# Three quarters of w_down in seven block products in place of eight

## The chip, the cores and the metric

The kernel runs on one core of one Trainium2 chip. The metric is the device time of one execution in microseconds; of several runs the median counts. The engines are TensorE (PE), VectorE (DVE), ScalarE (ACT), GpSimd (POOL) and SyncE (SP); matmuls write to PSUM, everything else of the work lies in SBUF, and weights come from HBM by DMA.

## The reference

One step of a hybrid decoder layer for 512 prompt tokens and 8 x 4 sample tokens (544 columns in all): two recurrent branches, a gated merge, an output projection, then an MLP and a last norm. Only the MLP is touched.

```python
D_MODEL = 1024
D_FF = 4 * D_MODEL
...
    h2 = _rmsnorm(x, norm_mlp_g)
    x = x + jnp.square(jax.nn.relu(h2 @ w_up)) @ w_down
...
    y = _rmsnorm(x, norm_final_g)
```

All data is float32.

## The kernel before

Activations lie channel-major: a tile has 128 channels on the partitions and the 544 tokens as columns, in two halves of 272 (HALF). To keep float32 accuracy every operand is split into two parts for the matmul, hi (rounded, by ACT) and lo (the difference, by DVE), and a product is the sum of three: hi x hi, lo x hi, hi x lo.

The unit of work is `full_unit`: `load8` (SP, L177) brings 128 columns of a weight, [128, 8, 128] = 512 KB, into a stage tile `st` (4 buffers), `split` makes `whi` (ACT, L132, 3 buffers) and `wlo` (DVE, L135, 2 buffers), and 48 matmuls (L129: 3 pairs of parts x 8 tiles of 128 rows x 2 halves of the columns) fill one `pd` tile, which has two PSUM banks. The pool of these has two tiles, so the next unit runs while this one is read out.

The MLP goes through the hidden rows in two halves and a rest. For each of e = 0, 1 there are 16 up units; of each DVE makes `r` = max(ps, 0) * rsb (L138, one operation for each half of the columns), ACT squares it and makes `hd` hi, DVE `hd` lo. Then come the products with w_down for 8 output tiles x2[j] of 128 channels (names x in the trace): in e = 0 two units of 8 hidden tiles each, in e = 1 one unit, and DVE adds the sum to x2[j] (two operations of 272). The last quarter of the hidden rows (3072 and up) follows apart: its weights are kept as `wkh`, `wkl`, and each part of the tokens is finished with the last norm while the next products run.

So w_down takes 24 units of 48 matmuls for the first three quarters. Each engine runs its instructions in the order of its own stream; waits between engines are semaphores. Loads are issued by SP as soon as a stage buffer is free.

Of the kernel before, what the change touches and what calls it, by code (L numbers as in the profile page):

```python
# [20 lines left out]
NSMP = NB * NT  # L21
# [15 lines left out]
NS_M = 43  # L37
# [23 lines left out]
def hybrid_step(ctx: ExitStack, tc: tile.TileContext, i, o):  # L61
# [47 lines left out]
    class Lane:  # L109
        """slots and PSUM banks of one of the two background lanes"""  # L110
# [32 lines left out]
    def rsq(x, scale=None, eps=None):  # L143
        """x <- (x * scale + eps) ** -0.5 of a few columns: a guess from the exponent, three Newton steps"""
# [67 lines left out]
    def stats(t):  # L212
        """1 / rms of every token of a tile, on every partition"""
# [52 lines left out]
    class Late:  # L266
        """Pool operations that stay behind those already queued"""
# [17 lines left out]
    def consts1():  # L285
# [5 lines left out]
        # masks of the RWKV pair products, rows s, columns t: [A_vk^T | A_re^T] over [A_zb^T (negated) | A_rb^T]  # L291
# [27 lines left out]
    def consts3():  # L319
        # sample masks: same sequence, strictly causal towards kk, causal towards r  # L320
# [9 lines left out]
        # rows of a sequence: bmk[row, b]  # L330
# [216 lines left out]
    def rw_batch(pairs, xk, xr, xv):  # L547
        """channel-major preparation and the pair products of two head pairs"""
# [211 lines left out]
    def rw_chain(g):  # L760
        """the state from chunk to chunk, and the outputs"""
# [57 lines left out]
    def gn(y, ng, S):  # L819
        """zero mean, unit variance over the 64 values of each (token, head); y: [128, ng, 64]"""  # L820
# [31 lines left out]
    def rw_state(L, p):  # L852
        """sample states of a head pair, transposed to [(h, key), b, value]"""
# [12 lines left out]
    def rw_sample(L):  # L866
        """four tokens of eight sequences; rows (head of the pair, key side | value side, token)"""
# [297 lines left out]
    def hg_sample(L):  # L1165
        """four tokens of eight sequences, four heads; columns and rows (head, sequence, token)"""
# [27 lines left out]
        # exact parts stacked along the rows: k = [hi; lo; hi], v = [hi; hi; lo]  # L1194
# [180 lines left out]
    psm = ctx.enter_context(tc.tile_pool(name="psm", bufs=2, space=bass.MemoryType.PSUM))  # L1375

# [52 lines left out]
    def row_scale():  # L1429
        """1/sqrt(mean + eps) of every token on every partition"""  # L1430
# [96 lines left out]
    for e in range(2):  # L1527
        hd_hi, hd_lo = [], []
        for f in range(16):
            ps = full_unit(i["w_up"][0], 2048 * e + 128 * f, xg_hi, xg_lo,  # L1530
                           late=2 * (e == 0 and f == 0))[:, :, 0:HALF]
            if e == 0 and f == 0:
                row_scale()
            r = Y(TOK, name="r")
            for b in range(2):
                stt(r[:, HALF * b:HALF * b + HALF], ps[:, b], 0.0, rsb[:, HALF * b:HALF * b + HALF], ALU.max, ALU.mult)
            act(r, r, AF.Square)
            for c, hd in enumerate((hd_hi, hd_lo)):
                slot = M if f < 9 else O if 2 * f + c < 18 + NS_O else Y
                hd.append(slot(TOK, F32R, "hd"))  # L1540
            act(hd_hi[f], r)
            tt(hd_lo[f], r, hd_hi[f].bitcast(F32), ALU.subtract)
# [69 lines left out]
```

## Time and profile before

| | |
|---|---|
| median of 3 runs | 1001.56 us (999.77 to 1001.76) |
| span of the profiled execution, first to last instruction | 996.1 us |
| PE busy | 962.8 us, 97% |
| DVE busy | 584.3 us, 59% |
| ACT busy | 394.0 us, 40% |
| POOL busy | 135.8 us, 14% |

The profiled execution is known by its span alone; the runs' times are some 5 us above it. The stages from 560 us on are, by the chain that ended last: up units to 692, w_down of e = 0 to 789, up units of e = 1 to 885, then w_down of e = 1 and the last quarter. A busy share is an average over stages; what matters for the change are the stages from 604 to 934 us.

### The profile page before, as it was taken

To read this page: it belongs to the slowest core of one execution; us is meant where nothing else is said; L and a number is where in the kernel's file an instruction comes from. 1 tells how busy PE (TensorE), PEld (TensorE's weight loads), DVE (VectorE), ACT (ScalarE), POOL (GpSimd) and SP (SyncE) were. 2 spreads that over 40 slices of the span, in tenths; PEclk is the share of its full clock that TensorE was granted. 3 is DMA by queue.
4 is the path that set the end of the run, shared out by engine and by line. 5 is a ranking of instruction groups with operands and counts; after the bars stand their busy time and mean duration, and the time that the engine had idled before them with its cause. 6 is when DMAs were issued, how large, how long until landed. Compare 5 with 4: busy or idle time off the path is not lost.

```text
span 996.1 us, 21327 instructions
## 1 busy us (share of the span) xinstructions
PE 962.8 (97%) x8868; PEld 908.1 (91%) x8868; DVE 584.3 (59%) x1198; ACT 394.0 (40%) x722; POOL 135.8 (14%) x328
## 2 busy tenths in 40 slices
PE   5999999999999899999999999999999999999996
PEld 4999988889998886888899999999999999999995
DVE  6635979578696854679878554444222244445333
ACT  7554545514636441334444333333111233333232
POOL 4486423221132101101000000000000000000000
PEclk9999999999999899999999999999999999999998
DMA  9632343222345232445743642322223332234111
GB/s 273 173 105 81 81 91 100 57 66 90 114 107 109 44 107 63 124 135 171 256 122 128 197 128 84 87 85 86 85 86 89 97 90 86 86 106 142 50 44 48
DMA packets 191091, 106.38 MB, mean 107 GB/s; under 512 B 38945, under 2 KB 179047, under 8 KB 190994
## 3 DMA queue, kind: packets, MB, share of 16 engines
q1 hardware_dynamic: 165424, 95.16, 32.8%
q10 hardware_dynamic: 25570, 9.85, 3.9%
q8 instruction: 70, 1.15, 0.5%
q14 instruction: 27, 0.22, 0.1%
HBM read 85.08 MB, written 18.39 MB: 104 GB/s over the span
## 4 chain that ended last, share of the span: by engine, by line
PE 81%; DVE 9%; DMA 4%; ACT 3%; POOL 2%; issue 1%; SPq 1%; ACTq 0%; DVEq 0%; POOLq 0%
PE pd L129 24%; PE in_unit_ps L129 20%; PE full_unit_ps L129 19%; PE half_unit_ps L129 4%; PE rw_chain_pq L129 2%; DVE tmp L135 2%; PE rw_chain_py L129 1%; DVE wlo L135 1%; PE rw_out_pt L129 1%; PE rw_sample_pn L129 1%; PE hg_head_po L129 1%; PE lora_ps L129 1%; DVE bn L724 1%; DMA xin<-in_x_prompt_dram 1%; PE hg_head_pl L129 1%
## 5 line engine op out<-in xcount | busy, mean ns | idle before, releaser
L132 ACT ACTIVATE whi<-st 128x1024 fp32r<-128x1024 f32 x120 | 126.7, 1057 | 251.6 <-PE pd L129 119.2
L135 DVE TENSOR_TENSOR wlo<-st,whi 128x1024 fp32r<-128x1024 f32 x120 | 149.2, 1244 | 126.0 <-PE full_unit_ps L129 40.3
L129 PE MATMUL in_unit_ps<-h_hi,whi 128*128 128x272 f32 (+3 forms) x736 | 121.3, 300 | 2.3 <-ACT h_hi L132 1.4
L129 PE MATMUL in_unit_ps<-h_hi,wlo 128*128 128x272 f32 (+3 forms) x736 | 121.7, 299 | 0.0
L129 PE MATMUL in_unit_ps<-h_lo,whi 128*128 128x272 f32 (+3 forms) x736 | 121.2, 300 | 0.0
L129 PEld LDWEIGHTS in_unit_ps<-h_hi,whi 128*128 128x128 f32 x736 | 103.3, 194 | 8.4 <-issue 3.4
L129 PE MATMUL full_unit_ps<-hd,whi 128*128 128x272 f32 (+2 forms) x832 | 110.3, 289 | 0.0
L129 PEld LDWEIGHTS in_unit_ps<-h_hi,wlo 128*128 128x128 f32 x736 | 103.2, 193 | 4.4 <-issue 2.4
L129 PEld LDWEIGHTS in_unit_ps<-h_lo,whi 128*128 128x128 f32 x736 | 103.7, 194 | 3.8 <-issue 1.9
L129 PEld LDWEIGHTS full_unit_ps<-hd,whi 128*128 128x128 f32 x832 | 106.5, 188 | 0.0
L129 PE MATMUL pd<-xgl,whi 128*128 128x272 f32 x512 | 70.2, 289 | 0.0
L129 PE MATMUL pd<-xgh,wlo 128*128 128x272 f32 x512 | 69.8, 288 | 0.0
L129 PE MATMUL pd<-xgh,whi 128*128 128x272 f32 x512 | 69.8, 288 | 0.0
L141 POOL TENSOR_SCALAR ys<-ys,ssf 32x512 f32<-32x512 f32 x1 | 0.8, 830 | 491.1 <-DVE ssf L1495 491.1
L129 PEld LDWEIGHTS pd<-xgl,whi 128*128 128x128 f32 x512 | 66.7, 188 | 0.0
L129 PEld LDWEIGHTS pd<-xgh,whi 128*128 128x128 f32 x512 | 66.2, 188 | 0.0
L129 PEld LDWEIGHTS pd<-xgh,wlo 128*128 128x128 f32 x512 | 66.2, 188 | 0.0
L129 PE MATMUL full_unit_ps<-hd,wlo 128*128 128x272 f32 (+2 forms) x416 | 56.8, 288 | 0.0
L129 PEld LDWEIGHTS full_unit_ps<-hd,wlo 128*128 128x128 f32 x416 | 54.0, 188 | 0.0
L135 DVE TENSOR_TENSOR hd<-r,hd 128x544 fp32r<-128x544 f32 x32 | 23.2, 725 | 47.9 <-ACT hd L132 47.9
L135 DVE TENSOR_TENSOR x<-x,full_unit_ps 128x272 f32<-128x272 f32 (+2 forms) x48 | 19.5, 434 | 36.9 <-PE full_unit_ps L129 36.9
L138 DVE SCALAR_TENSOR_TENSOR r<-pd,rsb 128x272 f32<-128x272 f32 x64 | 25.2, 435 | 25.9 <-PE pd L129 23.9
(413 smaller groups left out, 1500.9 us busy)
## 6 DMA issues: line engine op xcount, KB each, us to landing
st<-in_w_in_dram SPq DMA_DIRECT2D x46, 512.0 KB
st<-in_w_up_dram SPq DMA_DIRECT2D x32, 512.0 KB
st<-in_w_down_dram SPq DMA_DIRECT2D x32, 512.0 KB
gt_d<-gt SPq DMA_DIRECT2D x16, 272.0 KB
st<-in_w_out_dram SPq DMA_DIRECT2D x8, 512.0 KB
gtb<-gt_d SPq DMA_DIRECT2D x8, 272.0 KB
gta<-gt_d SPq DMA_DIRECT2D x8, 272.0 KB
x<-xt_d SPq DMA_DIRECT2D x8, 272.0 KB
```

The lines of the kernel that those rows point to most:

```text
L129: T.matmul(out, lhsT, rhs, start=start, stop=stop)
L132: A.activation(out=out, in_=in_, func=func, **kw)
L135: (eng or V).tensor_tensor(out=out, in0=a, in1=b, op=op)
L138: V.scalar_tensor_tensor(out=out, in0=a, scalar=s, in1=b, op0=op0, op1=op1)
L141: (eng or V).tensor_scalar(out=out, in0=a, scalar1=s1, scalar2=s2, op0=op0, op1=op1)
L724: V.tensor_reduce(out=o_[:, i0:i1, t0:t1], in_=tp, axis=AX.X, op=ALU.add)
```

## The change

The three quarters of the hidden rows 0 to 3071 are taken one after the other. Within a quarter each pair of hidden tiles (two of 128 rows), each pair of output tiles and the two halves of the tokens make a product of 2 x 2 blocks, and this is done by the scheme of Winograd with seven block products and sums of operands in place of eight. A block product is 12 matmuls of 272 columns (3 pairs of parts x 4 hidden pairs), and `down(c, ops, jp)` does the seven products for quarter c and output pair jp: 84 matmuls where there were 96.

- The sums of activations (`bt`, `t23`, `t4`) are made in `even` and `odd` behind the up units, and their parts take the place of those of the plain hidden values.
- The sums of weights (`sx`, in place in `st`, `s4`) are made in `down_weights` from two loads: t2 (odd hidden tiles) and t1 (even ones), each in two DMAs of 256 KB on SP. w1, w3 and w4 are split by ACT and DVE as before. Of w2, which is t2 as loaded, ACT makes hi, then a negated copy of it in the new tile `slo`, and a DMA issued by POOL adds t2 to that copy.
- Products 1 and 5 share a `pd` tile, 6 and 7 the next; these sums are kept over the quarters in `acc` (eight tiles of 544), written by ACT in c = 0 and added to by DVE after. Products 2 and 3 are added to one x2 tile at once, product 4 is subtracted from the other. Once, with c = 2, `combine(jp)` brings the kept sums into x2 by six DVE operations.
- One up unit of the next quarter runs ahead of the downs of each quarter.
- The last quarter (`plain`, and what follows) is as before. Pools: NS_M from 43 to 44, a pool `sp` for `slo` (2) and `sx` (1), `gs` moved to another pool. Docstrings and comments are left out.

```diff
-    for e in range(2):
-        hd_hi, hd_lo = [], []
-        for f in range(16):
...
-        for j in range(8):
-            ps = pd("full_unit_ps")
-            for kb in range(2 - e):
-                full_unit(i["w_down"][0], 128 * j, hd_hi[8 * kb:8 * kb + 8], hd_lo[8 * kb:8 * kb + 8], ps,
-                          kb == 0, kb == 1 - e, 2048 * e + 1024 * kb)
-            for b in range(2):
-                r = slice(HALF * b, HALF * b + HALF)
-                tt(x2[j][:, r], x2[j][:, r], ps[:, b, 0:HALF], ALU.add)
...
+    def even(r):
+
+        bt, t23 = Y(TOK, name="bt"), Y(TOK, name="t23")
+        act(bt[:, lh], r[:, lh], AF.Square)
+        act(t23[:, rh], r[:, rh], AF.Square)
+        tt(bt[:, rh], t23[:, rh], bt[:, lh], ALU.subtract)
+        return bt, t23
+
+    def odd(c, k, r, bt, t23, p0, H):
+
+        b2 = Y(TOK, name="b2")
+        act(b2, r, AF.Square)
+        tt(t23[:, rh], b2[:, rh], t23[:, rh], ALU.subtract)
+        tt(t23[:, lh], b2[:, rh], bt[:, rh], ALU.subtract)
+        p2 = parts(c, b2)
+        t4 = Y(HALF, name="t4")
+        tt(t4, t23[:, lh], b2[:, lh], ALU.subtract)
+        p3 = parts(c, t23)
...
+        return {1: cut(p0, lh), 5: cut(p0, rh), 2: cut(p2, lh), 3: cut(p2, rh), 6: cut(p3, lh), 7: cut(p3, rh),
+                4: cut(H, q)}
...
+    def down_weights(c, jp):
+
+        src = i["w_down"][0][1024 * c:1024 * c + 1024].rearrange("(k h p) c -> p h k c", h=2, p=128)
+        t = []
+        for h in (1, 0):
+            st = pipe.tile([128, 1024], F32, tag="stage", name=nm("st"), bufs=NST)
+            for r in range(2):
+                nc.sync.dma_start(out=st[:, 512 * r:512 * r + 512].rearrange("p (k c) -> p k c", k=4),
+                                  in_=src[:, h, :, 256 * jp + 128 * r:256 * jp + 128 * r + 128])
+            t.append(st)
+        t2, t1 = t
+        w2 = W()
+        w2.hi = pipe.tile([128, 1024], F32R, tag="whi", name=nm("whi"))
+        w2.lo = sp.tile([128, 1024], F32R, tag="slo", name=nm("slo"), bufs=NS_L)
+        act(w2.hi, t2)
+        act(w2.lo, w2.hi.bitcast(F32), AF.Copy, scale=-1.0)
+        P.dma_start(out=w2.lo, in_=t2, accum_op=ALU.add)
+        sx = sp.tile([128, 1024], F32, tag="sx", name=nm("sx"))
+        u, v = slice(0, 512), slice(512, 1024)
+        tt(sx[:, v], t1[:, u], t1[:, v], ALU.subtract)
+        tt(t1[:, v], t1[:, v], t2[:, v], ALU.add)
+        w1 = split(t1)
+        tt(sx[:, u], t1[:, v], t1[:, u], ALU.subtract)
+        w3 = split(sx)
+        s4 = t1[:, u]
+        tt(s4, t2[:, u], sx[:, u], ALU.subtract)
...
+        return {1: cut(w1, 0), 5: cut(w1, 512), 6: cut(w3, 0), 7: cut(w3, 512), 2: cut(w2, 0), 4: cut(w2, 512),
+                3: cut(w4, 0)}
+
+    def down(c, ops, jp):
...
+            seq = {0: ((0, 0), (0, 1), (1, 0)), 1: ((1, 0), (0, 0), (0, 1))}[first]
...
+        for q, (m0, m1) in enumerate(((1, 5), (6, 7))):
+            ps = pd("full_unit_ps")[:, :, 0:HALF]
+            product(m0, ps[:, 0], 0)
+            product(m1, ps[:, 1], 0)
+            if c:
+                tt(h2(acc[jp][q]), h2(acc[jp][q]), ps, ALU.add)
+            else:
+                act(h2(acc[jp][q]), ps)
+        xa, xb = x2[2 * jp], x2[2 * jp + 1]
+        p4, ps = ph("full_unit_ps")[:, 0:HALF], pd("full_unit_ps")[:, :, 0:HALF]
+        product(2, ps[:, 0], 0)
+        product(4, p4, 1)
+        tt(xb[:, lh], xb[:, lh], p4, ALU.subtract)
+        product(3, ps[:, 1], 0)
+        tt(h2(xa), h2(xa), ps, ALU.add)
...
+    r0 = None
+    for c in range(3):
+        ops, H = [], []
+        for f in range(8):
+            if f % 2 == 0:
+                bt, t23 = r0 if f == 0 and c else even(up_unit(c, f))
+                p0 = parts(c, bt)
+            else:
+                ops.append(odd(c, f // 2, up_unit(c, f), bt, t23, p0, H))
+        r0 = up_unit(c + 1, 0)
+        if c < 2:
+            r0 = even(r0)
+        for jp in range(4):
+            down(c, ops, jp)
+    plain(r0)
+    for f in range(1, 8):
+        plain(up_unit(3, f))
+        if f < 5:
+            combine(f - 1)
```

Where the instructions stand is told at three places, all in the products with w_down (of before in e = 0; of after in c = 1, where output pair jp = 0 goes over to jp = 1). `full_unit_ps` are PSUM tiles, `hd` parts of activations, numbers tell one tile from another.

On PE, before, two matmuls in a row read the same weights (x2, one for each bank):

```order
2044 L129 MATMUL full_unit_ps_8912<-hd_7915,wlo_8916 128x272 x2
2045 L129 MATMUL full_unit_ps_8912<-hd_7978,wlo_8916 128x272 x2
2046 L129 MATMUL full_unit_ps_8912<-hd_8041,wlo_8916 128x272 x2
2047 L129 MATMUL full_unit_ps_8912<-hd_8104,wlo_8916 128x272 x2
2048 L129 MATMUL full_unit_ps_8912<-hd_8167,wlo_8916 128x272 x2
```

and after, from the last matmul of product 3 on (`wlo_9628` is w4.lo) through product 1 of the next pair (`whi_9737` and `wlo_9738` are w1):

```order
2484 L130 MATMUL full_unit_ps_9684<-hd_9408,wlo_9628 128x272
2485 L130 MATMUL full_unit_ps_9751<-hd_8915,whi_9737 128x272
2486 L130 MATMUL full_unit_ps_9751<-hd_9058,whi_9737 128x272
2487 L130 MATMUL full_unit_ps_9751<-hd_9199,whi_9737 128x272
2488 L130 MATMUL full_unit_ps_9751<-hd_9342,whi_9737 128x272
2489 L130 MATMUL full_unit_ps_9751<-hd_8916,whi_9737 128x272
2490 L130 MATMUL full_unit_ps_9751<-hd_9059,whi_9737 128x272
2491 L130 MATMUL full_unit_ps_9751<-hd_9200,whi_9737 128x272
2492 L130 MATMUL full_unit_ps_9751<-hd_9343,whi_9737 128x272
2493 L130 MATMUL full_unit_ps_9751<-hd_8915,wlo_9738 128x272
```

Each matmul now fills one bank with weights of its own, and the lo weights are first read by the ninth matmul of the product.

On ACT, before, the products with w_down bring one `whi` for each unit and nothing else:

```order
561 L132 ACTIVATE whi_8969<-st_8967 128x1024
562 L132 ACTIVATE whi_9026<-st_9024 128x1024
563 L132 ACTIVATE whi_9080<-st_9078 128x1024
564 L132 ACTIVATE whi_9137<-st_9135 128x1024
565 L132 ACTIVATE whi_9191<-st_9189 128x1024
```

and after, w2.hi, its negated copy `slo`, then w1.hi, w3.hi and w4.hi of one pair, and the first three of the next:

```order
618 L133 ACTIVATE whi_9609<-st_9603 128x1024
619 L133 ACTIVATE slo_9610<-whi_9609 128x1024
620 L133 ACTIVATE whi_9617<-st_9606 128x1024
621 L133 ACTIVATE whi_9622<-sx_9614 128x1024
622 L133 ACTIVATE whi_9627<-st_9606 128x512
623 L133 ACTIVATE whi_9729<-st_9723 128x1024
624 L133 ACTIVATE slo_9730<-whi_9729 128x1024
625 L133 ACTIVATE whi_9737<-st_9726 128x1024
```

Five copies stand for a pair of output tiles and a quarter where two stood. In the pool of three `whi` tiles, w1.hi of a pair takes the buffer that w2.hi of the pair before it had, and waits for its last reader, product 4.

On DVE, before, two `wlo` and the two updates of an x2 tile alternate:

```order
903 L135 TENSOR_TENSOR x_7367<-x_7367,full_unit_ps_9023 128x272 x2
904 L135 TENSOR_TENSOR wlo_9249<-st_9246,whi_9248 128x1024
905 L135 TENSOR_TENSOR wlo_9303<-st_9300,whi_9302 128x1024
906 L135 TENSOR_TENSOR x_7432<-x_7432,full_unit_ps_9134 128x272 x2
907 L135 TENSOR_TENSOR wlo_9360<-st_9357,whi_9359 128x1024
```

and after, one pair's work, from the update by product 4:

```order
992 L136 TENSOR_TENSOR x_7305<-x_7305,full_unit_ps_9563 128x272
993 L136 TENSOR_TENSOR wlo_9618<-st_9606,whi_9617 128x1024
994 L136 TENSOR_TENSOR x_7242<-x_7242,full_unit_ps_9564 128x544
995 L136 TENSOR_TENSOR wlo_9623<-sx_9614,whi_9622 128x1024
996 L136 TENSOR_TENSOR st_9606<-st_9603,sx_9614 128x512
997 L136 TENSOR_TENSOR acc_7766<-acc_7766,full_unit_ps_9631 128x544
998 L136 TENSOR_TENSOR sx_9734<-st_9726 128x512
999 L136 TENSOR_TENSOR wlo_9628<-st_9606,whi_9627 128x512
1000 L136 TENSOR_TENSOR st_9726<-st_9726,st_9723 128x512
1001 L136 TENSOR_TENSOR sx_9734<-st_9726 128x512
1002 L136 TENSOR_TENSOR acc_7767<-acc_7767,full_unit_ps_9657 128x544
```

The sums and parts of the next pair's weights now stand between the readings of PSUM; in c = 2 the six operations of a combine stand in the same stream.

## Rows read from the trace of the kernel before

**Rows 1.** The page, busy us, share of the span and instructions of each engine.

```profile
PE 962.8 (97%) x8868; PEld 908.1 (91%) x8868; DVE 584.3 (59%) x1198; ACT 394.0 (40%) x722; POOL 135.8 (14%) x328
```

**Rows 2.** Chain of waits: start us, us, what, with its count.

```profile
692.36 96.35 PE full_unit_ps L129 x768
788.71 96.44 PE pd L129 x768
...
939.36 2.84 PE full_unit_ps L129 x24
```

**Rows 3.** Busy us of each engine by stretch, clock, DMA share, GB/s.

```profile
692.00:788.00 96.00, 96.00 (x767) 96.00 (x766) 26.58 (x33) 18.18 (x18) 0.00 (x0) 1.00 0.31 88
789.00:885.00 96.00, 96.00 (x767) 96.00 (x766) 42.84 (x63) 34.79 (x46) 0.00 (x0) 1.00 0.31 89
```

**Rows 4.** Timeline of PE in the branch projection: start us, us, what.

```profile
530.76 0.67 PE L129 MATMUL half_unit_ps<-oh,whi 128*128 128x272 f32 x4
...
542.84 0.67 PE L129 MATMUL half_unit_ps<-oh,whi 128*128 128x272 f32 x4
```

**Rows 5.** Groups of DVE, 600 to 940: busy us, mean ns, idle before.

```profile
L135 DVE TENSOR_TENSOR wlo<-st,whi 128x1024 fp32r<-128x1024 f32 x56 | 68.6, 1225 | 107.7 <-PE full_unit_ps L129 40.3 <-issue 33.0 <-PE pd L129 30.0
...
L135 DVE TENSOR_TENSOR hd<-r,hd 128x544 fp32r<-128x544 f32 x32 | 23.2, 725 | 47.9 <-ACT hd L132 47.9
L135 DVE TENSOR_TENSOR x<-x,full_unit_ps 128x272 f32<-128x272 f32 x32 | 12.5, 432 | 8.0 <-PE full_unit_ps L129 8.0
L135 DVE TENSOR_TENSOR wkl<-st,wkh 128x512 fp32r<-128x512 f32 x12 | 7.9, 689 | 8.8 <-ACT wkh L132 7.7 <-PE full_unit_ps L129 1.1
```

**Rows 6.** Groups of ACT, 600 to 940, in the same columns.

```profile
L132 ACT ACTIVATE whi<-st 128x1024 fp32r<-128x1024 f32 x55 | 58.3, 1060 | 214.7 <-PE pd L129 117.2 <-PE full_unit_ps L129 94.5 <-DMA st<-in_w_down_dram 2.9
L132 ACT ACTIVATE hd<-r 128x544 fp32r<-128x544 f32 x32 | 21.1, 659 | 1.0
...
L132 ACT ACTIVATE wkh<-st 128x512 fp32r<-128x512 f32 x12 | 6.9, 625 | 10.6 <-DMA st<-in_w_down_dram 9.2 <-PE full_unit_ps L129 1.4
```

**Rows 7.** Groups of DVE, 560 to 600: the update from PSUM in one operation.

```profile
L135 DVE TENSOR_TENSOR x<-x,pd 128x544 f32<-128x544 f32 x6 | 4.3, 722 | 4.6 <-PE pd L129 4.6
```

**Rows 8.** Timeline around the end of an up unit, all engines.

```profile
613.84 2.17 PE L129 MATMUL pd<-xgh,whi 128*128 128x272 f32 x16
614.05 0.79 DVE L138 SCALAR_TENSOR_TENSOR r<-pd,rsb 128x272 f32<-128x272 f32 x2 [0.80 <-PE pd L129]
614.05 1.06 ACT L132 ACTIVATE whi<-st 128x1024 fp32r<-128x1024 f32 x1 [3.65 <-PE pd L129]
615.01 0.64 ACT L132 ACTIVATE r<-r 128x544 f32<-128x544 f32 x1
615.68 0.66 ACT L132 ACTIVATE hd<-r 128x544 fp32r<-128x544 f32 x1
...
616.38 0.72 DVE L135 TENSOR_TENSOR hd<-r,hd 128x544 fp32r<-128x544 f32 x1 [1.54 <-ACT hd L132]
```

**Rows 9.** Timeline of ACT and DVE where weights of the last quarter come in.

```profile
912.49 1.16 ACT L132 ACTIVATE wkh<-st 128x512 fp32r<-128x512 f32 x2 [2.08 <-DMA st<-in_w_down_dram]
...
914.63 1.16 ACT L132 ACTIVATE wkh<-st 128x512 fp32r<-128x512 f32 x2 [0.99 <-DMA st<-in_w_down_dram]
...
915.91 1.22 DVE L135 TENSOR_TENSOR wlo<-st,whi 128x1024 fp32r<-128x1024 f32 x1
917.04 0.69 DVE L135 TENSOR_TENSOR wkl<-st,wkh 128x512 fp32r<-128x512 f32 x1
917.64 0.78 DVE L135 TENSOR_TENSOR x<-x,full_unit_ps 128x272 f32<-128x272 f32 x2
```

**Rows 10.** Timeline of SP: issues of the loads that rows 9 wait for.

```profile
908.35 0.37 SPq L177 DMA_DIRECT2D st<-in_w_down_dram  x1
...
909.49 0.37 SPq L177 DMA_DIRECT2D st<-in_w_down_dram  x1
```

**Rows 11.** Groups of POOL, 500 to 990 us.

```profile
L141 POOL TENSOR_SCALAR ys<-ys,ssf 32x512 f32<-32x512 f32 x1 | 0.8, 830 | 491.1 <-DVE ssf L1495 491.1
```

More of the change, by code (lines that the diff above doesn't have):

```diff
@@ L36 @@
 NS_O = 12
-NS_M = 43
+NS_M = 44
+NS_L = 2
 NST = 4
@@ L1524, in final @@
         put(1, nc.scalar)
-    for e in range(2):
-        hd_hi, hd_lo = [], []
-        for f in range(16):
[L1530 to L1534, printed above, removed]
-            for b in range(2):
[L1536 to L1542, printed above, removed]
-        for j in range(8):
-            ps = pd("full_unit_ps")
-            for kb in range(2 - e):
-                full_unit(i["w_down"][0], 128 * j, hd_hi[8 * kb:8 * kb + 8], hd_lo[8 * kb:8 * kb + 8], ps,
-                          kb == 0, kb == 1 - e, 2048 * e + 1024 * kb)
-            for b in range(2):
-                r = slice(HALF * b, HALF * b + HALF)
-                tt(x2[j][:, r], x2[j][:, r], ps[:, b, 0:HALF], ALU.add)
@@ new lines, in hybrid_step, with hd, parts, up_unit @@
+    lh, rh = slice(0, HALF), slice(HALF, TOK)
+    slots = {}
+    def hd(c):
+        n = slots[c] = slots.get(c, -1) + 1
+        if c == 3:
+            return (M if n < 2 else O if n < 2 + NS_O else Y)(TOK, F32R, "hd")
+        return (O if n < NS_O else M if n < NS_O + 10 else Y)(TOK, F32R, "hd")
+    def parts(c, v):
+        hi, lo = hd(c), hd(c)
+        act(hi, v)
+        tt(lo, v, hi.bitcast(F32), ALU.subtract)
+        return hi, lo
+    def up_unit(c, f):
+        ps = full_unit(i["w_up"][0], 1024 * c + 128 * f, xg_hi, xg_lo,
+                       late=2 * (c == 0 and f == 0))[:, :, 0:HALF]
+        if c == 0 and f == 0:
+            row_scale()
+        r = Y(TOK, name="r")
+        for b in range(2):
+            stt(r[:, HALF * b:HALF * b + HALF], ps[:, b], 0.0, rsb[:, HALF * b:HALF * b + HALF], ALU.max, ALU.mult)
+        return r
@@ new lines, in even @@
+    def even(r):
[13 more added lines that the diff above has]
+        p3 = parts(c, t23)
+        if k % 2 == 0:
+            H[:] = [hd(c), hd(c)]
+        q = (lh, rh)[k % 2]
+        act(H[0][:, q], t4)
+        tt(H[1][:, q], t4, H[0][:, q].bitcast(F32), ALU.subtract)
+        cut = lambda p, h: [v[:, h] for v in p]
+        return {1: cut(p0, lh), 5: cut(p0, rh), 2: cut(p2, lh), 3: cut(p2, rh), 6: cut(p3, lh), 7: cut(p3, rh),
+                4: cut(H, q)}
@@ new lines, in hybrid_step @@
+    acc = [[M(TOK, name="acc") for _ in range(2)] for _ in range(4)]
+    def down_weights(c, jp):
[23 more added lines that the diff above has]
+        tt(s4, t2[:, u], sx[:, u], ALU.subtract)
+        w4 = W()
+        w4.hi = pipe.tile([128, 1024], F32R, tag="whi", name=nm("whi"))[:, u]
+        w4.lo = pipe.tile([128, 1024], F32R, tag="wlo", name=nm("wlo"), bufs=2)[:, u]
+        act(w4.hi, s4)
+        tt(w4.lo, s4, w4.hi.bitcast(F32), ALU.subtract)
+        cut = lambda w, a: [[x[:, a + 128 * k:a + 128 * k + 128] for k in range(4)] for x in (w.hi, w.lo)]
+        return {1: cut(w1, 0), 5: cut(w1, 512), 6: cut(w3, 0), 7: cut(w3, 512), 2: cut(w2, 0), 4: cut(w2, 512),
+                3: cut(w4, 0)}
@@ new lines, in down, with product @@
+    def down(c, ops, jp):
+        w = down_weights(c, jp)
+        def product(m, ps, first):
+            seq = {0: ((0, 0), (0, 1), (1, 0)), 1: ((1, 0), (0, 0), (0, 1))}[first]
+            n = 0
+            order = [(s, k) for s in seq for k in range(3)] + [(s, 3) for s in seq] if jp == 0 else \
+                [(s, k) for s in seq for k in range(4)]
+            for (a, b), k in order:
+                mm(ps, w[m][a][k], ops[k][m][b], n == 0, n == 11)
+                n += 1
+        for q, (m0, m1) in enumerate(((1, 5), (6, 7))):
[13 more added lines that the diff above has]
+        tt(h2(xa), h2(xa), ps, ALU.add)
@@ new lines, in combine, with plain @@
+    def combine(jp):
+        xa, xb = x2[2 * jp], x2[2 * jp + 1]
+        a, b = acc[jp]
+        tt(xa, xa, a, ALU.add)
+        tt(b[:, lh], b[:, lh], a[:, lh], ALU.add)
+        tt(b[:, rh], b[:, rh], b[:, lh], ALU.add)
+        tt(xa[:, rh], xa[:, rh], b[:, lh], ALU.add)
+        tt(h2(xb), h2(xb), bc(b[:, rh], 1, 2), ALU.add)
+        tt(xb[:, rh], xb[:, rh], a[:, rh], ALU.add)
+    hd_hi, hd_lo = [], []
+    def plain(r):
+        act(r, r, AF.Square)
+        hi, lo = parts(3, r)
+        hd_hi.append(hi)
+        hd_lo.append(lo)
@@ L1574, in hybrid_step @@
                 for k in range(8):
-                    mm(ps, w[k], x[8 + k][:, r], s == 0 and k == 0, s == 2 and k == 7)
+                    mm(ps, w[k], x[k][:, r], s == 0 and k == 0, s == 2 and k == 7)
             if e or j:
```

3 lines of the change are left out of this document (2 added, 1 removed).

## The prediction, made before the changed kernel had run

> **What bounds the kernel now.** I read the busy times of the engines first, then the chain of waits from 560 us on, then a table of busy time by stage, then single groups and a few stretches of timeline in the stage that changes. TensorE (PE) is busy 97% of the span [rows 1]. From 560 us on the chain that ended last is PE alone: rows of PE follow each other without a gap, 692.36 + 96.35 = 788.71, and so on up to the last quarter [rows 2]. The reader is to see that nothing else ever ends a wait there. In the stage of the first w_down products (692 to 788) PE is busy 96.00 of 96 us at a granted clock of 1.00 (the 2.4 GHz level), and VectorE (DVE) only 26.58, ScalarE (ACT) 18.18; the next up stage has PE 96.00 as well, DVE 42.84, ACT 34.79 [rows 3]. So in the changed stage a matmul taken away is time taken away, one for one, as long as DVE, ACT and the weight transfers keep up. They have slack there; the change spends it.
>
> **What is removed.** Per pair of output tiles and quarter of the hidden rows there were 8 block products of 12 matmuls (3 pairs of parts x 4 tiles), and there are 7 now. Over 4 pairs and 3 quarters: 12 x 96 = 1152 matmuls before, 12 x 84 = 1008 now, all 128x272. Before, 768 of them took 96.35 us [rows 2], so 0.12546 us each; 1152 are 144.5 us. The new ones fill one PSUM bank each, with other weights at every matmul, where before two matmuls shared their weights. The nearest row for that form is the branch projection, half_unit_ps: 24 groups of four from 530.76 to 542.84 are 96 matmuls in 12.08 us, 0.1258 each [rows 4]. So 1008 cost 126.5 us at the old pitch, 126.8 at the one-bank pitch. **Saving 17.7 to 18.1 us; I take 17.9.** The up units are 32 before and after, and the last quarter has the same matmuls: nothing.
>
> **What is added, on ACT and DVE.** One down (84 matmuls) is 84 x 0.1254 = 10.53 us on PE. With T = 0 at its start, products 1 and 5 run to 3.0, 6 and 7 to 6.0, 2 to 7.5, 4 to 9.03, 3 to 10.53. In that time ACT prepares the next one's weights: four copies of 1024 columns (w2.hi, w2.lo, w1.hi, w3.hi) at 1.06 and one of 512 at 0.63 [rows 6], 4.9 us; in the first quarter two copies of sums more (0.66 each, the price of the 544-column hd [rows 6]). It fits. DVE has two lo parts of 1024 at 1.225, one of 512 and four sums of 512 at 0.69, and one x update of 272 at 0.43 [rows 5]; two accumulations and one x update of 544 from PSUM at 0.72 [rows 7]: 2.45 + 3.45 + 0.43 + 2.16 = 8.5 us of 10.53. Queued back to back the pitch is shorter than the durations (915.91, 917.04, 917.64: 1.13 for a 1.22 row, 0.60 for a 0.69 row [rows 9]), which makes it 7.6. It fits too, with 2 to 3 us to spare. In the third quarter the scheduler has put the six operations of each combine between the downs' work on DVE: two of 544 and four of 272, 2 x 0.72 + 4 x 0.43 = 3.1 us more [rows 5], so 10.4 to 11.6 us in the downs where they fall, which is at the bound or 1.1 us over it.
>
> **The one tight chain.** Three whi buffers serve four hi parts per down. w1.hi of the next down takes the buffer of w2.hi, so it waits for the end of product 4, at 9.03. From there: 0.20 to the start on ACT (matmul 613.84, ACT 614.05 [rows 8]), 1.06 for w1.hi, 0.04 to DVE (ACT's hd ends at 616.34, DVE starts at 616.38 [rows 8]), 1.225 for w1.lo = 11.56; PE's own crossing is bounded by the 0.20 in the other direction, so 11.76. The first matmul that reads w1.lo is the ninth of product 1: 10.53 + 8 x 0.1254 = 11.53. PE waits about 0.2 us. The first down of a quarter has its weights made under the up units, so this is for 3 x 3 = 9 downs: 1.8 us. In the third quarter combine sits in front of the same w1.lo; by the two DVE sums this is from nothing to about 0.9 us in each of 3 downs. Sum 1.8 to 4.5 us; **I take 3**, nearer the middle, since neither pitch is the rule on DVE in the rows.
>
> **The transfer that accumulates.** w2.lo is made by ACT (minus w2.hi) and then a DMA issued by GpSimd (POOL) adds the 512 KB of t2 to it. The last POOL row before the very end lies 491 us back [rows 11]: POOL's queue is free, and no row shows a transfer of this kind. Bounds: a plain load of 512 KB takes from its issue (908.35) to the first use (912.49) 4.1 us, behind another (909.49 to 914.63) 5.1 us [rows 9, 10]. An accumulating one reads both sides and writes one; if these went one after the other it would be three times as much, 12.3 to 15.4 us. The cover: ACT has the negated copy ready at 7.85 (8.5 in the first quarter), and product 2 of the next down reads w2.lo with its ninth matmul, at 10.53 + 0.2 + 6.0 + 1.0 = 17.7. That leaves 9.2 to 9.9 us. I take a duration of 5 to 8 us, nearest the plain rows since the bytes written are the same: hidden, at no cost. Its POOL instruction waits for ACT, with nothing queued behind it but the next of its kind.
>
> No run here shows it, but the Trainium skill says that per-element accumulation needs a transfer issued from GpSimd (DMA: Bandwidth & Descriptors, "SWDGE vs HWDGE vs iDMA"), and fits such a transfer by 2.0 us plus bytes over 436e3 per us (the same page, "Anatomy of one DMA — SWDGE (gpsimd) path"): an estimate of 3.2 us for 512 KB, without a word on what the accumulation adds. By it the sum stays as it is.
>
> **The plain loads.** t2 and t1 now come in four transfers of 256 KB in place of two of 512 KB, the same bytes in 10.53 us in place of 12.0. t1 is issued when its stage buffer comes free, about 5.7, by the 4 to 5 us above it lands by 11, and its last half is first read for a product near 15: hidden. If it came over 4 us later, that would cost its excess in each down.
>
> **The up stages.** Per pair of up units (12 us of PE) DVE gets three lo parts of 544, one of 272 and four sums of 272 beside two times the old r (0.79) and wlo: 3 x 0.72 + 5 x 0.43 + 2 x 0.79 + 2 x 1.225 = 8.3 us [rows 5, 8]; ACT, with the same copies as before and one of 272 more, under 6. Hidden, and PE runs an up unit of the next quarter ahead of the downs, which covers the building of the last operands. Where the last up unit ends and the last quarter begins, 0.2 + 0.79 + 0.64 + 0.66 of r, square and hi [rows 6, 8], about 2.3 us, stand beside 21 matmuls of the last quarter that PE does first (24 of them took 2.84 [rows 2], so 2.5): hidden. The tail behind it is unchanged.
>
> **Sum.** The span of 996.1 less 17.9 plus 3.0 is 981.2. The median of the runs shown lies 5.5 us above the span; I carry that over: 981.2 + 5.5 = 986.7 us.
>
> **Rivals.**
> - *Everything hidden.* DVE runs at its back-to-back pitch, and PE's crossing is shorter than 0.2. For it: DVE's short rows in rows 9. Stalls 0 to 1 us: 983.5 to 984.7.
> - *The weight chain costs more.* Around 1 us instead of 0.2 in each of 9 downs, and 1 to 2 us in those with combine: DVE has 11 separate operations per down, most with a wait on ACT, PE or a load, and POOL's issuing work may hold up DVE. The nearest price is a POOL row of 0.83 us [rows 11]; nine or twelve times that is 7.5 to 10 us: 989 to 998. Against it: DVE's 2 us of slack lie outside the chain from product 4 to w1.lo, if POOL's work does too.
> The Trainium skill has a rule for this: a DVE instruction with two SBUF inputs contends with a GpSimd instruction that reads SBUF (SBUF — State Buffer, "Who interferes with whom"). All lo parts have two such inputs; no row here shows both engines at once.
> - *The accumulation is slow (the other side).* If the transfer takes X > 9.9 us from its issue to its use, product 2 of the next down stalls X - 9.9. The stall itself gives the following transfer that much more time, so it alternates: two of the three downs of a quarter that need it, 6 x (X - 9.9) in all. The gain of 14.9 us is gone at X = 12.4. At X = 14 it is 24.6 us: 1011; at the bound of 15.4 it is 33: 1020. For it: the three-fold bound above. Against: DMA engines were a third busy in this stage (share 0.31 [rows 3]).
> - *The change does nothing for PE*: one-bank matmuls with new weights each time could run slower. For no change they would have to cost 0.143 us each; rows 4 says 0.126. Hardly any chance.
>
> **How the numbers follow.** Forecast with stalls of 1.2 to 5 us (984.7 to 989): 0.50. Everything hidden: 0.20. The weight chain costs more (989 to 998): 0.18. No gain within 0.2% (2 us, about what a measurement of this kernel can tell from no change): 0.03. Slow accumulation: 0.09. The range takes the first two and most of the third, 983 to 996, with 0.15 or so left out. Faster by over 0.2%: 0.50 + 0.20 + 0.18 = 0.88; within: 0.03; slower: 0.09.
>
> **What would show it.** PE's count falls by 144 and its busy time by about 18 us. Right: between products 3 and 1 of the downs PE waits some 0.2 us for DVE's w1.lo, and for nothing else. Wrong: rows of PE released by a DMA on slo (then the transfer's time from POOL's issue decides), by ACT's w1.hi, or by DVE's acc; DVE rows much longer than 1.225 or 0.69 while POOL issues; one-bank matmuls above 0.126.

## The result and the profile after

The changed kernel took 988.4 us (median), the kernel before 1001.2 beside it; the ratio is 0.988 with an interval of 0.984 to 0.992. Two more comparisons gave 986.8 against 999.3 (0.987, 0.985 to 0.990) and 987.4 against 997.7 (0.989, 0.986 to 0.992). The forecast was 986.7, a gain of 14.9 us; the gains measured are 12.8, 12.6 and 10.3 us. (The first profile of the changed kernel fell into a disturbed execution of 2105 us; the rows here are of its profile in the second comparison, named e1_again.)

The page answers [rows 1]: PE has 144 matmuls fewer and is busy 18.6 us less, DVE 85 us more, ACT 51 more.

```profile
PE 944.2 (96%) x8724; PEld 887.8 (90%) x8724; DVE 669.2 (68%) x1362; ACT 444.9 (45%) x802; POOL 146.3 (15%) x340
```

The chain of waits (start us, us, what) answers [rows 2]. It is to be read by stages: pieces of `full_unit_ps` are the three rounds of downs, 336 matmuls each; pieces of `pd` are up units.

```profile
601.71 45.27 PE pd L130 x359
646.97 42.66 PE full_unit_ps L130 x336
689.64 48.24 PE pd L130 x384
737.88 42.54 PE full_unit_ps L130 x336
780.42 48.21 PE pd L130 x384
828.63 27.00 PE full_unit_ps L130 x212
855.70 1.07 ACT whi L133
856.79 1.07 ACT slo L133
...
858.15 4.51 DMA slo<-st
862.71 9.81 PE full_unit_ps L130 x76
872.52 10.06 PE pd L130 x80
```

The rounds take 42.66, 42.54 and (828.63 to 872.52) 43.89 us, 129.1 in all; 1152 matmuls at the old pitch were 144.5. So the downs gave 15.4 us, what was forecast for the whole (14.9). But from the end of the norm's statistics to the end of the span, the only stretch in which the two programs differ, before took 996.1 - 604.88 = 391.2 us and the changed kernel 983.6 - 601.71 = 381.9: a gain of 9.3. Some 6 us were given back after the downs. (The stretch ahead of it, in which the two programs have the same instructions, took from 602 to 610 us in the profiles here. That difference between executions is as large as the gain, so the stages are compared below.)

The table by stage answers [rows 3]: busy us of PE, PEld, DVE, ACT, POOL, then clock, DMA share, GB/s, for the three rounds of downs.

```profile
647.00:689.00 42.00, 42.00 (x333) 41.62 (x332) 25.14 (x35) 23.14 (x30) 2.57 (x3) 1.00 0.55 140
738.00:780.00 42.00, 42.00 (x334) 41.65 (x333) 30.16 (x43) 19.53 (x23) 2.56 (x3) 1.00 0.57 142
829.00:872.00 43.00, 41.94 (x332) 41.48 (x331) 38.91 (x63) 19.11 (x21) 2.58 (x3) 1.00 0.55 135
```

DVE has 30.2 us of work in the second round, 7.5 per down (forecast 7.6 to 8.5), and 38.9 in the third. Cut at 839.5, 850 and 860.5 us, which is about where one down ends and the next begins, the third has 8.3, 10.2, 10.5 and 10.5 us of it (the last in 12 us, with PE's wait); forecast were 10.4 to 11.6 for downs with a combine. So DVE is nearly as full there as forecast.

The 6 us stand here, in the timeline where the last up unit (`pd`, to 914.5) goes over to the last quarter:

```profile
911.64 1.06 ACT L133 ACTIVATE whi<-st 128x1024 fp32r<-128x1024 f32 x1 [2.13 <-DMA st<-in_w_down_dram]
...
914.55 2.64 PE L130 MATMUL full_unit_ps<-hd,wkh 128*128 128x256 f32 x21
914.61 1.29 DVE L136 TENSOR_TENSOR wkl<-st,wkh 128x512 fp32r<-128x512 f32 x2
915.82 1.22 DVE L136 TENSOR_TENSOR wlo<-st,whi 128x1024 fp32r<-128x1024 f32 x1
916.95 1.29 DVE L136 TENSOR_TENSOR wkl<-st,wkh 128x512 fp32r<-128x512 f32 x2
918.15 0.79 DVE L139 SCALAR_TENSOR_TENSOR r<-pd,rsb 128x272 f32<-128x272 f32 x2
918.97 0.66 ACT L133 ACTIVATE r<-r 128x544 f32<-128x544 f32 x1 [3.47 <-DVE r L139]
919.66 0.66 ACT L133 ACTIVATE hd<-r 128x544 fp32r<-128x544 f32 x1
...
920.37 0.58 PE L130 MATMUL full_unit_ps<-hd,wkh 128*128 128x256 f32 x1 [3.17 <-ACT hd L133]
```

PE does the 21 matmuls that can go first and then waits 3.17 us for the hi part of the last hidden tile. The up unit was done at 914.5, and r could have started then; but r stands in DVE's stream behind five weight parts of the last quarter, 914.61 to 918.15. Then the granted clock falls to the lower of its two levels for some 6 us (the same columns as above):

```profile
914.00:917.00 3.00, 3.00 (x27) 2.99 (x25) 3.00 (x5) 1.50 (x3) 0.00 (x0) 1.00 0.00 0
917.00:920.30 3.30, 0.20 (x2) 0.00 (x0) 1.94 (x5) 1.30 (x2) 0.00 (x0) 0.88 0.00 0
920.40:924.00 3.60, 3.60 (x17) 3.60 (x18) 0.68 (x1) 0.00 (x0) 0.00 (x0) 0.50 0.02 5
924.00:926.00 2.00, 2.00 (x11) 2.00 (x11) 0.42 (x1) 0.00 (x0) 0.00 (x0) 0.50 0.00 0
```

In the chain the next 34 matmuls take 6.96 us; where the clock stayed at 1.00 they take 4.26 to 4.29. So 3.17 + 2.7 = 5.9 us, and 15.4 - 5.9 = 9.5, against 9.3 measured.

### The profile page after: what moved, and what is told of

Same layout as the page of the kernel before. It is cut to its first block, busy times and chain, and to the rows that moved or that the text cites. A ratio compares the mean times of both kernels' runs of the same rounds, so it can differ in the third digit from the quotient of the medians.

```text
span 2103.4 us, 21378 instructions
## 1 busy us (share of the span) xinstructions
PE 2085.9 (99%) x8724; PEld 1957.8 (93%) x8724; DVE 679.2 (32%) x1362; ACT 446.7 (21%) x802; POOL 128.3 (6%) x340
## 4 chain that ended last, share of the span: by engine, by line
PE 99%; DMA 0%; ACT 0%; issue 0%; SPq 0%; DVE 0%; ACTq 0%
PE in_unit_ps L130 34%; PE pd L130 27%; PE full_unit_ps L130 18%; PE half_unit_ps L130 6%; PE rw_chain_pq L130 2%; PE rw_batch_pa L130 1%; PE rw_chain_py L130 1%; PE lora_ps L130 1%; PE rw_sample_pn L130 1%; PE hg_head_po L130 1%; PE hg_head_pl L130 1%; PE rw_out_pt L130 1%; PE rw_sample_pz L130 1%; PE head_sums_ps L130 0%; PE rw_batch_pt L662 0%; PE hg_head_pk L130 0%
## 5 line engine op out<-in xcount | busy, mean ns | idle before, releaser
L136 DVE TENSOR_TENSOR wlo<-st,whi 128x1024 fp32r<-128x1024 f32 (+1 forms) x120 | 140.8, 1173 | 427.9 <-PE in_unit_ps L130 179.3
L130 PE MATMUL in_unit_ps<-h_hi,wlo 128*128 128x272 f32 (+3 forms) x736 | 265.7, 549 | 0.0
L130 PE MATMUL in_unit_ps<-h_hi,whi 128*128 128x272 f32 (+3 forms) x736 | 264.5, 548 | 0.0
L130 PE MATMUL in_unit_ps<-h_lo,whi 128*128 128x272 f32 (+3 forms) x736 | 264.4, 549 | 0.0
L133 ACT ACTIVATE whi<-st 128x1024 fp32r<-128x1024 f32 (+1 forms) x132 | 134.0, 1016 | 604.2 <-PE pd L130 282.8
L130 PEld LDWEIGHTS in_unit_ps<-h_hi,whi 128*128 128x128 f32 x736 | 231.8, 379 | 13.6 <-issue 12.4
L130 PEld LDWEIGHTS in_unit_ps<-h_hi,wlo 128*128 128x128 f32 x736 | 234.0, 373 | 11.1 <-issue 9.6
L130 PEld LDWEIGHTS in_unit_ps<-h_lo,whi 128*128 128x128 f32 x736 | 233.4, 376 | 9.2 <-issue 7.7
L130 PE MATMUL full_unit_ps<-hd,whi 128*128 128x272 f32 (+2 forms) x736 | 219.6, 483 | 0.0
L130 PEld LDWEIGHTS full_unit_ps<-hd,whi 128*128 128x128 f32 x736 | 204.0, 329 | 0.5
L1602 POOL DMA_DIRECT2D slo<-st x12 | 10.5, 872 | 829.7 <-ACT slo L133 829.7
```

Source lines behind the costliest of these rows:

```text
L130: T.matmul(out, lhsT, rhs, start=start, stop=stop)
L133: A.activation(out=out, in_=in_, func=func, **kw)
L136: (eng or V).tensor_tensor(out=out, in0=a, in1=b, op=op)
L1602: P.dma_start(out=w2.lo, in_=t2, accum_op=ALU.add)
```

## The experiments

**The changed kernel again**, for the profile above, and once more beside the last two kernels.

> The changed kernel as it is, for a profile at the usual clock. Theory (small stalls): 985 to 989 us; PE idles some 3 us in all between the first and the last product with w_down, most of it in front of the ninth matmul of product 1, waiting for DVE's w1.lo. Rival 1 (the weight chain is long): 9 us of idle there. Rival 2 (the accumulating transfer is in the way): idle in front of the ninth matmul of product 2, released by a DMA.

986.8 us. PE has two waits between 600 and 930 us that are recorded as idle, the one for hd and one in the third round; the view is the waits of PE (us in total, times, longest):

```profile
PE full_unit_ps L130 <- ACT hd L133: 3.2, 1, 3.2
PE full_unit_ps L130 <- DMA slo<-st: 1.1, 1, 1.1
```

The forecast stall in front of w1.lo is there too, but as a stretched pitch and not as idle. PE's timeline at the start of a second down: eight matmuls with w1.hi from 657.38, the four with w1.lo from 658.46, the next from 659.07.

```profile
657.38 1.17 PE L130 MATMUL full_unit_ps<-hd,whi 128*128 128x272 f32 x8
658.46 0.78 PE L130 MATMUL full_unit_ps<-hd,wlo 128*128 128x272 f32 x4
659.07 1.17 PE L130 MATMUL full_unit_ps<-hd,whi 128*128 128x272 f32 x8
```

Twelve matmuls in 1.69 us in place of 1.50: 0.19 us, where 0.2 was forecast. The rival with 1 us per down falls.

> The changed kernel again, beside the next two on the same chip. By its stages: 42.7, 42.5 and 43.9 us for the three rounds of downs, a wait of about 3.2 us before the last quarter, with or without a fall of the granted clock behind it: 985 to 989 us.

987.4 us, with the rounds at 42.66, 42.55 and 43.89 us, the same within a hundredth. The wait before the last quarter was 1.5 us this time, and the clock stayed up (4.26 us for the 34 matmuls).

```profile
920.40 2.64 PE L130 MATMUL full_unit_ps<-hd,wkh 128*128 128x256 f32 x21
...
924.53 0.39 PE L130 MATMUL full_unit_ps<-hd,wkh 128*128 128x256 f32 x1 [1.49 <-ACT hd L133]
```

The last weights had landed earlier by the up unit's time: ACT's whi began 4.6 us ahead of the end of the up unit and not 2.9. So the size of this wait hangs on when a load lands, and differs between executions. From the statistics to the end it took 377.5 us, a gain of 13.7: 17.9 less 2.7 in the downs and 1.5 there.

**w1.hi waits for an earlier product.**

```diff
-        w4.hi = pipe.tile([128, 1024], F32R, tag="whi", name=nm("whi"))[:, u]
-        w4.lo = pipe.tile([128, 1024], F32R, tag="wlo", name=nm("wlo"), bufs=2)[:, u]
+        w4t = pipe.tile([128, 1024], F32R, tag="wlo", name=nm("wlo"), bufs=2)
+        w4.hi, w4.lo = w4t[:, v], w4t[:, u]
```

> One edit: w4.hi lies in the unused half of w4.lo's tile, so that the three whi tiles serve three hi parts per down and w1.hi waits for the end of product 7 (6.0 us into the down) in place of product 4 (9.0). Theory: the stall in front of w1.lo goes, 2 to 3 us faster than the changed kernel. Rival 1: 9 us faster. Rival 2, or stalls that lie elsewhere: no difference.

986.0 us against 999.3 of before; the runs scatter too much to tell it from the changed kernel by its median. The chain of waits does tell:

```profile
654.38 42.15 PE full_unit_ps L130 x336
...
744.77 42.00 PE full_unit_ps L130 x336
...
834.99 42.23 PE full_unit_ps L130 x336
```

The rounds are 126.4 us, 2.7 less than 129.1, and 126.38 / 1008 is 0.1254 per matmul, the old pitch: hardly a stall is left in them (the second is 42.00 us, the others 0.15 and 0.23 longer), though each combine is still there. The forecast of 126.5 for 1008 matmuls holds, and the stalls were 2.7 where 3 was taken. With the waits for w1.lo the one for `slo` is gone as well; with this edit the scheduler puts PE's matmuls in another order (that of the changed kernel is shown below, at the kernel without combine). The wait before the last quarter was 2.1 us, and the clock fell behind it.

**144 matmuls put back.** Product 3 is made twice.

```diff
         product(3, ps[:, 1], 0)
+        product(3, ps[:, 1], 0)
```

> Product 3 is made twice, the second over the first: 12 x 12 = 144 matmuls more, as many as the change took away, and 1.5 us more cover for w1.lo in each down. Theory: 144 x 0.1255 = 18.1 us less the stalls of about 3 that this covers, so 15 us slower than the changed kernel and within 1 to 3 us of the kernel before. Rival 1 (9 us of stalls): 9 us slower than the changed kernel, well under the kernel before. If matmuls in this form cost more than 0.126 us, above 18 us.

1001.2 us against 999.3 of before, 14.5 above the changed kernel (15 forecast). The rounds of 384 matmuls take 48.15, 48.09 and 48.24 us, 0.1254 each, without a stall: the 1.5 us of cover per down are enough. From the statistics to the end it takes 1001.6 - 609.9 = 391.7, as before did (391.2), with all the added work on ACT, DVE and POOL. So what the change gains is the price of the 144 matmuls, and the added work alone costs 0.5 us at most where each down has this cover.

**Without combine.**

```diff
-        if f < 5:
-            combine(f - 1)
```

> The six DVE operations for each output pair that bring the kept sums into x2 are left out, so the output lacks products 1, 5, 6 and 7. Theory: 0.5 to 2.7 us faster than the changed kernel, by the stalls of the third quarter. Rival: no difference, since DVE has slack for them.

984.3 us against 999.3. The three rounds are 42.68, 42.57 and 42.71 us: the third is 1.2 us shorter than with combine, and like the others now. But what went is the wait for `slo`, not time of DVE. Why the changed kernel has that wait, its order on PE shows. In the last down of the third quarter two matmuls of product 4 (`full_unit_ps_10966`) stand among those of products 1 and 6, the first of them as the ninth of the down:

```
3077 L130 MATMUL full_unit_ps_10914<-hd_10391,whi_10900 128x272
3078 L130 MATMUL full_unit_ps_10966<-hd_10039,slo_10893 128x272
3079 L130 MATMUL full_unit_ps_10940<-hd_10035,whi_10905 128x272
```

So w2.lo is wanted 1.0 us into this down in place of 7.0. The transfer was issued at 858.15 and landed after 4.51 us; PE came to this matmul at 861.65. Without combine, with product 3 twice, and with either of the edits to the weights (w4.hi above, w2.lo below), the scheduler leaves the products in their order, and the wait isn't there.

**w2.lo by DVE.**

```diff
-        act(w2.lo, w2.hi.bitcast(F32), AF.Copy, scale=-1.0)
-        P.dma_start(out=w2.lo, in_=t2, accum_op=ALU.add)
+        tt(w2.lo, t2, w2.hi.bitcast(F32), ALU.subtract)
```

> w2.lo is made by DVE from t2 and w2.hi, as any other lo part; the negated copy on ACT and the accumulating transfer are gone. Theory (the transfer of 4.5 us is hidden but for one down, DVE is the engine with the least slack): 1.225 us more on DVE in each of 12 downs, 9 to 10 us of 10.5 in the first two quarters and over the bound in the third; 1 to 4 us slower than the changed kernel. Rival (the transfer and its issue are what costs in the downs): 1 to 2 us faster.

984.9 us against 999.0: not slower than the changed kernel, so the expectation was wrong. The rounds are 42.66, 42.55 and 42.73 us, with DVE busy 40.45 of 42 us in the third and no recorded wait of PE there (columns as above):

```profile
835.00:877.00 42.00, 42.00 (x333) 41.65 (x332) 40.45 (x63) 16.19 (x18) 0.00 (x0) 1.00 0.36 102
```

DVE was 96% busy in this stage and held PE up no more than in the changed kernel: the stalls at w1.lo stay (42.7 us and not 42.0), and nothing is added to them. The wait for hd before the last quarter was 2.5 us, with the fall of the clock behind it (5.82 us for the 34 matmuls). No gain from the accumulating transfer shows here: from the statistics to the end this kernel took 986.7 - 607.95 = 378.8 us, between the 377.5 and 381.9 of the changed kernel.

**The accumulating transfer three times.**

```diff
         P.dma_start(out=w2.lo, in_=t2, accum_op=ALU.add)
+        P.dma_start(out=w2.lo, in_=t2, accum_op=ALU.add)
+        P.dma_start(out=w2.lo, in_=t2, accum_op=ALU.add)
```

> The accumulating transfer is made three times, one behind the other, so w2.lo holds minus w2.hi plus three times t2 (the output is off by that): from the first issue to the last landing some 13.5 us in place of 4.5. Theory (a cover of 9.2 to 9.9 us per down, every second of them stalling): 6 x 3.9 = 23 us slower than the changed kernel, with PE waiting for the transfer. Rival (every down stalls): 9 x 3.9 = 35 us. Rival (the cover is larger than worked out): under 10 us.

1043.7 us, 57 above the changed kernel, more than any of the three numbers. The timeline of PE, the matmuls with an idle time before them in the first two quarters and in the third:

```profile
676.18 2.18 PE L130 MATMUL full_unit_ps<-hd,slo 128*128 128x272 f32 x8 [8.67 <-DMA slo<-st]
...
708.91 2.18 PE L130 MATMUL full_unit_ps<-hd,slo 128*128 128x272 f32 x8 [7.52 <-DMA slo<-st]
787.63 2.18 PE L130 MATMUL full_unit_ps<-hd,slo 128*128 128x272 f32 x8 [8.24 <-DMA slo<-st]
802.12 1.27 PE L130 MATMUL full_unit_ps<-hd,slo 128*128 128x272 f32 x8 [2.16 <-DMA slo<-st]
817.55 1.81 PE L130 MATMUL full_unit_ps<-hd,slo 128*128 128x272 f32 x8 [3.74 <-DMA slo<-st]
...
895.86 2.18 PE L130 MATMUL full_unit_ps<-hd,slo 128*128 128x272 f32 x8 [7.63 <-DMA slo<-st]
909.07 1.27 PE L130 MATMUL full_unit_ps<-hd,slo 128*128 128x272 f32 x8 [0.50 <-DMA slo<-st]
926.46 2.18 PE L130 MATMUL full_unit_ps<-hd,slo 128*128 128x272 f32 x8 [5.66 <-DMA slo<-st]
```

The three transfers of the first wait ran from 658.51 (POOL's issue) to 676.18, 17.7 us and not 13.5: one takes 5.3 us in the median here, and up to 7.0 where it stands in the chain. The cover is 17.7 - 8.7 = 9.0 us in the first quarter, and 787.63 - 769.84 - 8.24 = 9.55 in the second: the forecast had 9.2 to 9.9. In the first quarter the second transfer of three has no wait, as the rival's alternation wants; in the others it has a small one. These waits are 44.1 us. The three rounds take 64.4, 61.4 and 61.7 us, 58.4 more than in the changed kernel: 43 of it are these waits (less the 1.1 that was there before), and the other 15 lie in the same rounds, where the matmuls behind a wait run at a longer pitch (8 of them in 2.18 us; 1.17 is usual). The granted clock there was 0.87 over 660 to 700 us and 0.77 over 700 to 715. So the theory of 23 us was wrong in two terms, three transfers took 17.7 us and not 13.5, and a wait cost more than its length.

**Lo parts of the last weights on POOL.** Of the lo parts in the last quarter those of outputs 4, 5 and 7 are made by POOL.

```diff
-                tt(lo, st[:, c], hi.bitcast(F32), ALU.subtract)
+                tt(lo, st[:, c], hi.bitcast(F32), ALU.subtract, eng=P if j > 3 else None)
...
-            w = split(st)
+            w = split(st, P if j == 7 else None)
```

> In the last quarter the lo parts of the weights of outputs 4, 5 and 7 are made by POOL in place of DVE, so that DVE has no weight part in front of r of the last up unit. Theory (PE's wait of 3.2 us at the start of the last quarter, and the lower clock behind it, come from the queue on DVE): the wait falls under 0.3 us, the clock stays at 1.00 there, 3 to 6 us faster than the changed kernel. Rival (the wait comes from the latency of the chain r, square, hi): the wait stays at 2 us or more. Rival (POOL is too slow): a new wait of PE for wkl or wlo in the last quarter.

983.0 us against 999.0. The timeline at the same place as above:

```profile
914.92 2.17 PE L130 MATMUL pd<-xgl,whi 128*128 128x272 f32 x16
915.39 2.56 POOL L136 TENSOR_TENSOR wkl<-st,wkh 128x512 fp32r<-128x512 f32 x2 [0.62 <-ACT wkh L133]
916.94 2.82 PE L130 MATMUL full_unit_ps<-hd,wkh 128*128 128x256 f32 x21
917.14 0.79 DVE L139 SCALAR_TENSOR_TENSOR r<-pd,rsb 128x272 f32<-128x272 f32 x2 [1.59 <-PE pd L130]
917.90 2.40 POOL L136 TENSOR_TENSOR wlo<-st,whi 128x1024 fp32r<-128x1024 f32 x1
917.96 0.66 ACT L133 ACTIVATE r<-r 128x544 f32<-128x544 f32 x1 [1.61 <-DVE r L139]
918.65 0.66 ACT L133 ACTIVATE hd<-r 128x544 fp32r<-128x544 f32 x1
919.35 1.53 DVE L136 TENSOR_TENSOR hd<-r,hd 128x544 fp32r<-128x544 f32 x1 [1.42 <-ACT hd L133]
919.59 1.11 PE L130 MATMUL full_unit_ps<-hd,wkl 128*128 128x256 f32 x8
```

r starts 0.20 us behind the up unit and PE doesn't wait; the clock stays up. The chain r, square, hi is as short as forecast, 916.94 to 919.31, and the 21 matmuls do cover it, if nothing stands in front of r on DVE. From the statistics to the end it takes 980.0 - 604.06 = 375.9 us. The rounds are those of the changed kernel.

**Both edits.**

> Both edits: w4.hi in the tile of w4.lo, and the three lo parts on POOL. Theory: no wait of PE left between 610 us and the tail, all of the 17.9 us of 144 matmuls gained: 5 to 8 us faster than the changed kernel, some 982 us. If the gains do not add: no better than the better of the two.

983.0 us against 999.0, by the median no faster than with the lo parts on POOL alone; the stages tell the two apart. No wait of PE is left but two in the tail, 0.8 us together, which the kernel before the change has too. From the statistics to the end it takes 977.8 - 604.54 = 373.3 us, where the lo parts on POOL alone gave 375.9: 17.9 less than before, the whole price of 144 matmuls.

> w4.hi in the tile of w4.lo and three outputs' lo parts on POOL. By the stages (42.2, 42.0, 42.2, no wait before the last quarter): 5.9 us faster than the changed kernel where its clock falls, 2.6 + 3.2 = 5.8 less 2.7 for what a kept clock would spare there, so 3 to 9 us.

Beside the changed kernel (987.4) and before (997.7) it took 979.9 us: 7.5 us faster than the changed kernel, 17.8 than before (0.982, 0.979 to 0.984). From the statistics to the end it takes 978.0 - 604.73 = 373.3 us again.

> The same, and w2.lo made by DVE in place of the accumulating transfer. If DVE still has slack (it had in the kernel with this edit alone): the downs at 42.0 to 42.3, the same time. If the shorter waits of ACT and PE bring DVE to its bound (9.7 us of work for 10.53, 12.8 with a combine): up to 2 us more in the third quarter.

981.7 us (0.983, 0.981 to 0.986). The rounds are 42.15, 42.00 and 42.23 us with DVE busy 41.5 of 42.1 us in the third: still no wait there. From the statistics to the end it takes 980.2 - 606.59 = 373.6 us, against 373.3 with the transfer; so, as far as one execution of each shows, most of the 1.8 us between the medians lies ahead of the stages that differ. At the start of the last quarter PE waits 0.2 us for the lo part of the last hidden tile, which took 2.32 us on DVE and not 0.72, beside POOL's wlo:

```profile
918.48 2.38 POOL L136 TENSOR_TENSOR wlo<-st,whi 128x1024 fp32r<-128x1024 f32 x1
919.12 2.32 DVE L136 TENSOR_TENSOR hd<-r,hd 128x544 fp32r<-128x544 f32 x1 [1.42 <-ACT hd L133]
```

## Why the prediction was right, and where it was not

The direction and the main mechanism held: 986.7 forecast, 986.8 to 988.4 measured. That one median lies within 0.1 us of the forecast is luck: in that comparison the gain was 2.3 us smaller than the 14.9 forecast, and the kernel before 2.2 us faster than the 1001.6 that the forecast started from. By the stages the changed kernel gained 9.3 and 13.7 us of the 17.9, so stalls and waits took 8.6 and 4.2 us where the sum has 3. Point by point:

- *144 matmuls at 0.1254 to 0.1258*: right. 0.1254 in the rounds without stalls, 17.9 us in all, and with them put back the time is that of the kernel before. The rows of the branch projection [rows 4] were the right ones for the new form; weights that change with every matmul cost nothing that shows here.
- *w1.lo*: right, 0.19 us per down where 0.2 was forecast; with an earlier buffer the stall is gone.
- *Combine*: over-sized. It was given up to 0.9 us in each of three downs. DVE is about as full as forecast, but with w4.hi in the other tile the third round, which has the combines, is 0.2 us longer than the second (42.23 and 42.00; 0.4 in one of the later runs, 42.41). The term was made from DVE's sum alone. That only work in front of w1.lo can hurt fits this, but no run puts it to the test.
- *The accumulating transfer*: it was a little shorter (4.5 us) than the 5 to 8 that were taken, and far from the 12.4 at which the gain would be gone; the cover was right, 9.0 to 9.6 us by the three-fold run. Wrong was that all downs have that cover. In the last down of the third quarter the matmuls stand in another order, which the listing of the order would have shown; it cost 1.1 us. A row of PE released by a DMA on slo is a sign that the prediction names for being wrong, and this one row bears it out. The Trainium skill's fit (DMA: Bandwidth & Descriptors, "Anatomy of one DMA — SWDGE (gpsimd) path") gives an estimate of 3.2 us for a transfer of these bytes issued by GpSimd; the accumulating one took 4.5.
- So the term of 3 us for stalls in the downs was met, 2.7, partly for another reason: 1.6 at w1.lo (126.4 to 129.1, less the 1.1) and 1.1 at slo.
- *The start of the last quarter*: wrong. The step said that 2.3 us of r, square and hi stand beside 2.5 us of matmuls, and that the tail is unchanged. Both lengths are right; what the step left out is the queue in front of r. Before, the weights of the last quarter were split while PE ran the w_down units of e = 1, and the hidden values were done. After, the same splits fall among the up units of the last quarter, five of them between the last two r on DVE, and the loads that they wait for decide when. The wait was 3.2 and 1.5 us in the two profiles of the changed kernel, and 2.7 us more where the clock fell behind it; with the lo parts on POOL it is gone.
- *The 5.5 us between span and median*: in every later run, which has both, the span lies 1.7 to 2.0 us under the time of its own execution. So the profiled execution of before was a faster one than the median (996.1 + 1.7 is some 997.8, an estimate), and the carry held a difference between executions that hides part of what the last quarter gave back.

The rival with 1 us per down fell by the pitch at w1.lo, that with a slow transfer by 4.5 us, that with dearer matmuls by 0.1254. The rival in which everything is hidden fell by the rounds (2.7 us of stalls); it is what both edits make of the kernel.

## What to carry to other kernels

When TensorE is full, fewer matmuls are worth their pitch. Here the sum of what other engines gained in work (85 us on DVE, 51 on ACT) mattered little; what mattered was each result that is wanted early, and what stands in front of it on its engine. Ask this at the seams too: if a change takes away the stage in which something was prepared at leisure, look where that preparation lands, operation by operation, on every queue. And read the order of the changed program at the last round of a loop, since a scheduler may treat it otherwise than the first.

## What the runs showed of the hardware

- After the wait of 3.17 us the granted clock of PE fell to 0.50, the lower of its two levels, for some 6 us. It fell behind the waits of 2.1 and 2.5 us in two other kernels too, later and for less long (5.82 us for the 34 matmuls in both), and not behind 2.6 us (without combine) and 1.5. So one such wait costs its length, or that and up to 2.7 us more.
- DVE beside POOL: the hd part of 544 took 1.53 us while POOL made a wlo (919.35 above) and 0.72 to 0.73 elsewhere, and POOL's wkl took 1.77 us there in place of 1.29. In the four kernels with lo parts on POOL this hd took 1.53, 1.98, 1.36 and 2.32 us, and in all four it ended 0.58 us behind the end of POOL's wlo (917.90 + 2.40 = 920.30 and 919.35 + 1.53 = 920.88 above). So by these rows it isn't slowed in proportion: it hardly gets on until POOL's operation is through, and its price is what is left of that. That agrees with the Trainium skill (SBUF — State Buffer, "Who interferes with whom"): a DVE instruction with two SBUF inputs contends with a GpSimd instruction that reads SBUF. POOL's issues of transfers showed no such cost: 0.86 us each on POOL, and DVE's wlo at 1223 ns beside 1225 before [rows 5].
- An accumulating transfer of 512 KB within SBUF took 4.5 us in the median from its issue on POOL to its landing, within the 4.1 to 5.1 of a plain load from issue to use [rows 9, 10].
